# Two FFN down products: two column blocks at once, their first k tiles through seven products

## The chip, the cores and the metric

The kernel runs on one core of a Trainium2 chip. The metric is the device time of one execution in microseconds (us), lower is better. A core has TensorE (PE, matmuls, with its weight loads shown as PEld), VectorE (DVE), ScalarE (ACT), GpSimd (POOL) and SyncE (SP, which issues most transfers). Each engine works through its own instructions in the order that the program gives it, and waits on semaphores for the others.

## The reference

One layer of a streaming encoder, 256 tokens, width 2048, f32. What this case touches are its two half-step FFNs (hidden width 5632):

```python
def swiglu(h, w_gate, w_up, w_down):
    return (jax.nn.silu(h @ w_gate) * (h @ w_up)) @ w_down

x = x + 0.5 * swiglu(rms_norm(x, ffn1_norm[i]), ffn1_w_gate[i], ffn1_w_up[i], ffn1_w_down[i])
...   # input projection, S5 group, stick-breaking attention group, output projection
x = x + 0.5 * swiglu(rms_norm(x, ffn2_norm[i]), ffn2_w_gate[i], ffn2_w_up[i], ffn2_w_down[i])
...   # per-layer embedding, gated
```

## The kernel before

Every f32 matrix product is made of three fp32r products. An operand is split into a high part (a cast on ScalarE, L168) and a low part (source minus high part, on VectorE, L171), by `split`; then high x high, low x high and high x low are summed in PSUM. Tokens are two tiles of 128 (`TT = 2`), weights come in "quarters" of four k tiles by one column block of 512 (`raw`, 1 MB, three buffers), split in two halves of two k tiles each (`whi`, `wlo`, four buffers each). One half against both token tiles is 12 matmuls with 512 columns, one quarter 24. `gemm_block` does this for one column block: for each quarter it asks `act` for the split activations, loads and splits the quarter's weights, and calls `gemm_half` for each half. `step()` after each half lets work that was put off go ahead (`put_off(n, f)` calls f after n steps).

`ffn` has two parts. Gate and up: for each of 11 blocks f of 512 hidden columns, both products over 16 k tiles, then silu(gate) * up goes to `hh` and is turned into `hT` by transposes on VectorE and transfers (`turned`). Down: four column blocks n, each over 44 k tiles (11 quarters) with `gemm_block`; its activations are split anew from `hT` for every quarter of every column block (`act`, two buffers `hhi`, `hlo`); the result is added to the residual `xt` (L594) and `nxt.block(n)`, which turns and splits x for the next norm, is put off.

FFN 2 has a second way for gate and up (`sevens`), from block f = 1 on: `gemm_seven` takes the first quarter of gate and of up together as a 2 x 2 block product (two token tiles, two pairs of k tiles, two column blocks) and makes it with seven block products in place of eight, in the form of Winograd. For that it needs weight sums t1 to t4 (L459, VectorE), four sums of activation blocks (`sum_forms`, L409 to L426, made once for all f), and combinations of the seven results, which are left to `opened` and `gated`. Each product p is 6 matmuls: 4 with the high part of the weights, 2 with the low part. The remaining quarters accumulate into the same PSUM banks. FFN 1 runs the preparation of the S5 group beside gate and up (`bg`), and has no `sevens`.

The kernel's instructions are put in order, engine by engine, when it is built (`pin` keeps some in the order written). The PSUM has four banks for `acc` and two double banks for `aux`. The buffer tag "h" (`com`) has two buffers and serves `hh`, `sum_forms` and the norm's turned blocks; tags "nhi"/"nlo" have four, "hhi"/"hlo" two.

Of the kernel before, what the change touches and what calls it, by code (L numbers as in the profile page):

```python
# [33 lines left out]
def layer_kernel(ctx: ExitStack, tc: tile.TileContext, a: dict, shapes: dict, out: bass.AP):  # L34
# [29 lines left out]
    def uid(s):  # L64
        count[0] += 1
        return f"{s}_{count[0]}"
# [13 lines left out]
    def acc(s="acc"):  # L80
        return accp.tile([P, NB], F32, tag="acc", name=uid(s))
# [83 lines left out]
    def split(hi, lo, src, scale=None, pinned=False):  # L165

        if scale is None:
            copy = nc.scalar.copy(hi, src)  # L168
            if pinned:
                pin(copy)  # L170
            nc.vector.tensor_tensor(out=lo, in0=src, in1=hi.bitcast(F32), op=ALU.subtract)  # L171
        else:
            split_each(hi.unsqueeze(1), lo.unsqueeze(1), src.unsqueeze(1), [scale])
# [251 lines left out]
        split(*both, sums.rearrange("p (z t) -> p z t", z=4))  # L425
        return both  # L426

    def gemm_seven(act, sums, ws, n0, nkt, pool, first, second):

        raws = []  # L430
        for w in ws:
            raw = wp.tile([P, 4, NB], F32, tag="raw", name=uid("raw"), bufs=3)
            nc.sync.dma_start(raw, w[: 4 * P, n0 : n0 + NB].rearrange("(j p) n -> p j n", p=P))
            raws.append(raw)
        b11, b21, b12, b22 = (raw[:, 2 * h : 2 * h + 2, :] for raw in raws for h in range(2))
        parts = act(0)

        def whole(k, t):
            return [[u[:, 2 * k + j, t * P : (t + 1) * P] for j in range(2)] for u in parts]

        def summed(z):
            return [[u[:, z, j * P : (j + 1) * P] for j in range(2)] for u in sums]

        def product(ps, left, src, own, stop):
            hi, lo = (
                (pool if own else wp).tile([P, 2, NB], F32R, tag=s, name=uid(s), bufs=3 if own else None)
                for s in (("shi", "slo") if own else ("whi", "wlo"))
            )
            split(hi, lo, src)
            lh, ll = left  # L450
            for j in range(2):
                nc.tensor.matmul(ps, lhsT=lh[j], rhs=hi[:, j], start=j == 0, stop=False)  # L452
                nc.tensor.matmul(ps, lhsT=ll[j], rhs=hi[:, j], start=False, stop=False)  # L453
            for j in range(2):
                nc.tensor.matmul(ps, lhsT=lh[j], rhs=lo[:, j], start=False, stop=stop and j == 1)  # L455

        def add(x, y):
            t = pool.tile([P, 2, NB], F32, tag="sum", name=uid("sum"), bufs=2)
            nc.vector.tensor_tensor(out=t, in0=x, in1=y, op=ALU.add)  # L459
            return t  # L460

        p1, p2 = acc(), acc()
        product(p1, whole(0, 0), b11, False, True)
        product(p2, whole(1, 0), b21, False, False)
        step()
        t1 = add(b11, b12)
        p5 = acc()
        product(p5, summed(0), t1, True, True)
        t2 = add(t1, b22)
        p67 = aux()  # L470
        product(p67[:, :NB], summed(1), t2, True, True)
        step()
        t4 = add(t2, b21)
        p4 = acc()
        product(p4, whole(1, 1), t4, True, False)
        t3 = add(b12, b22)
        product(p67[:, NB:], summed(2), t3, True, True)
        step()
        p38 = aux()
        product(p38[:, :NB], summed(3), b22, False, False)  # L480
        step()
        put_off(0, first, p1, p67)
        for w, banks, fresh in ((ws[0], [p2, p4], False), (ws[1], [p38[:, :NB], p38[:, NB:]], True)):
            for k0 in range(4, nkt, 4):
                part = act(k0 // 4)
                for half in list(weight_halves(w, k0, 4, n0)):
                    begin = k0 == 4 and half[0] == 0
                    end = k0 + 4 >= nkt and half[0] == 1
                    for t in range(TT):
                        gemm_half({t: banks[t]}, (part, half), (t,), fresh and t == 1 and begin, end)  # L490
                    step()
            if not fresh:
                put_off(0, second, p2, p4, p5)
        return p38

    def ffn(i, xn, nxt, bg=None):
        wg, wu, wd = (a[f"ffn{i}_w_{s}"][0] for s in ("gate", "up", "down"))
# [22 lines left out]
        for f in range(NF):  # L520
# [5 lines left out]
            if sevens and f:  # L526
                sg, hh = com("sg"), com("h")
                gate_cols, up_cols = ([u[:, t * NB : (t + 1) * NB] for t in range(TT)] for u in (sg, hh))

                def opened(p1, p67, g=gate_cols, u=up_cols):  # L530
                    nc.scalar.copy(g[0], p1)
                    nc.vector.tensor_tensor(out=u[0], in0=p67[:, :NB], in1=g[0], op=ALU.add)
                    nc.vector.tensor_tensor(out=u[1], in0=p67[:, NB:], in1=u[0], op=ALU.add)

                def gated(p2, p4, p5, g=gate_cols, u=up_cols, hh=hh):
                    for z, (ps, other) in enumerate(((p2, g[0]), (p4, u[1]))):
# [3 lines left out]
                    nc.vector.tensor_tensor(  # L540
                        out=v, in0=p5.unsqueeze(1).to_broadcast([P, TT, NB]), in1=v, op=ALU.subtract
                    )

                p38 = gemm_seven(xn, sums, (wg, wu), f * NB, KD, sevens, opened, gated)
                nc.vector.tensor_tensor(out=hh, in0=p38, in1=hh, op=ALU.add)
                for t in range(TT):
                    nc.vector.scalar_tensor_tensor(
                        out=up_cols[t], in0=up_cols[t], scalar=xn.rs(t), in1=gate_cols[t], op0=ALU.mult, op1=ALU.mult
                    )
                put_off(2, turned, hp, f, hh)  # L550
                continue
# [36 lines left out]
            split(in_32(hi), in_32(lo), hT[k // 2][:, k % 2 * 4 : k % 2 * 4 + 4])  # L588
            return hi, lo

        for n in range(ND):
            ps = gemm_block(act, wd, n * NB, F // P)
            for t in range(TT):
                nc.vector.scalar_tensor_tensor(  # L594
                    out=xt[t][n], in0=ps[t], scalar=0.5, in1=xt[t][n], op0=ALU.mult, op1=ALU.add
                )
            put_off(0 if n == ND - 1 and n < nxt.early else 2, nxt.block, n)
        pools.close()


# [950 lines left out]
```

## Time and profile before

| | |
|---|---|
| median of 3 runs | 1870.7 us (1870.19 to 1871.19) |
| the profiled execution | 1872.24 us, its span 1870.4 us |
| mean granted clock | 1.0 |
| HBM read / written | 369.26 MB / 9.83 MB |
| instructions in the span | 23938 |

Stages, from the trace: gate and up of FFN 1 until 490 us, down of FFN 1 until 730, the mixing groups until 1054, gate and up of FFN 2 until 1523, its down product until 1763, then the per-layer embedding.

How to read it: a row of the page gives line, engine, operation, out<-in by the program's names, shapes, a count, then busy time, mean ns of one, and the idle time of the engine just before them with what ended it. A row of the timeline gives start and length in us, and in brackets the idle time before it with its releaser. A window gives each engine's busy time, and near its end the granted TensorE clock (1.00 is full), the share of the DMA engines and GB/s.

### The profile page before, as it was taken

Reading aid. Unit: us, or ns where it says so; the run is one execution under the profiler, and the core shown is the slowest. Engines: PE = TensorE matmul, PEld = TensorE weight load, DVE = VectorE, ACT = ScalarE, POOL = GpSimd, SP = SyncE. Lnnn points to the kernel's source line nnn. Section 1 sums busy time; section 2 is a strip of 40 time slices with the busy share of each in tenths; the row PEclk is TensorE's granted clock in tenths of the full one; section 3 lists DMA queues with packets and bytes.
Section 4 is the critical chain, followed back from the end, with each engine's and each line's share of the span. In section 5 each row is a group of like instructions: output and inputs, shape, how many; then the busy total and the mean of one; then the engine's idle time right before and its main releaser. Section 6 shows DMA issues by size and latency. Waiting matters only on the chain.

```text
span 1870.4 us, 23938 instructions
## 1 busy us (share of the span) xinstructions
PE 1859.4 (99%) x9134; PEld 1536.3 (82%) x9134; DVE 1310.4 (70%) x1527; ACT 996.5 (53%) x1151; POOL 50.4 (3%) x84
## 2 busy tenths in 40 slices
PE   9999999999999999999999999999999999999998
PEld 7888888888888888878888888888888888888887
DVE  8867665455576776687567678778787866777655
ACT  7444444444456665456695555445454555666554
POOL 0011000000000000010020000000000000000000
PEclk9999999999999999999999999999999999999999
DMA  8788867766655666675645666575666675656563
GB/s 323 242 278 268 267 208 222 231 217 200 217 196 199 212 199 244 185 248 163 222 147 189 218 205 221 203 220 186 203 205 208 225 228 203 204 202 212 189 224 124
DMA packets 230387, 400.06 MB, mean 214 GB/s; under 512 B 26401, under 2 KB 50337, under 8 KB 229985
## 3 DMA queue, kind: packets, MB, share of 16 engines
q1 hardware_dynamic: 227824, 392.81, 63.7%
q0 software_dynamic: 1728, 4.33, 0.7%
q8 instruction: 71, 1.16, 0.3%
q10 hardware_dynamic: 720, 1.41, 0.2%
q14 instruction: 44, 0.35, 0.1%
HBM read 369.26 MB, written 9.83 MB: 203 GB/s over the span
## 4 chain that ended last, share of the span: by engine, by line
PE 92%; ACT 3%; DVE 2%; DMA 1%; SPq 1%; issue 1%; POOL 0%; DVEq 0%; ACTq 0%; POOLq 0%
PE acc L292 26%; PE acc L297 26%; PE acc L293 26%; PE aux L293 3%; PE aux L292 3%; PE aux L297 3%; ACT whi L168 1%; SPq L1061 1%; PE acc L455 1%; DMA raw<-in_w_in 1%; PE aux L452 1%; PE acc L452 1%; PE acc L453 1%; PE aux L455 1%; PE aux L453 1%
## 5 line engine op out<-in xcount | busy, mean ns | idle before, releaser
L171 DVE TENSOR_TENSOR wlo<-raw,whi 128x1024 fp32r<-128x1024 f32 x656 | 798.2, 1224 | 458.9 <-ACT whi L168 455.3
L168 ACT CAST whi<-raw 128x1024 fp32r<-128x1024 f32 x656 | 686.2, 1053 | 758.7 <-PE acc L293 607.9
L292 PE MATMUL acc<-whi,nhi 128*128 128x512 f32 x1408 | 551.0, 391 | 1.2 <-ACT whi L260 0.5
L293 PE MATMUL acc<-whi,nlo 128*128 128x512 f32 x1408 | 548.2, 389 | 0.0
L297 PE MATMUL acc<-wlo,nhi 128*128 128x512 f32 x1408 | 384.4, 389 | 0.0
L292 PE MATMUL acc<-whi,hhi 128*128 128x512 f32 x816 | 317.6, 389 | 0.0
L293 PE MATMUL acc<-whi,hlo 128*128 128x512 f32 x816 | 317.5, 389 | 0.0
L292 PEld LDWEIGHTS acc<-whi,nhi 128*128 128x128 f32 x1408 | 264.3, 188 | 58.3 <-ACT whi L168 1.7
L297 PEld LDWEIGHTS acc<-wlo,nhi 128*128 128x128 f32 x1408 | 264.2, 188 | 55.6 <-DVE wlo L171 0.4
L293 PEld LDWEIGHTS acc<-whi,nlo 128*128 128x128 f32 x1408 | 264.4, 188 | 54.0
L297 PE MATMUL acc<-wlo,hhi 128*128 128x512 f32 x816 | 221.0, 389 | 0.0
L297 PEld LDWEIGHTS acc<-wlo,hhi 128*128 128x128 f32 x816 | 152.8, 188 | 32.5 <-DVE wlo L171 0.9
L293 PEld LDWEIGHTS acc<-whi,hlo 128*128 128x128 f32 x816 | 153.2, 188 | 32.0
L292 PEld LDWEIGHTS acc<-whi,hhi 128*128 128x128 f32 x816 | 153.1, 188 | 31.8
L171 DVE TENSOR_TENSOR hlo<-hT,hhi 128x1024 fp32r<-128x1024 f32 x88 | 107.1, 1218 | 0.0
L168 ACT CAST hhi<-hT 128x1024 fp32r<-128x1024 f32 x88 | 91.8, 1044 | 0.5 <-PE acc L455 0.4
L292 PE MATMUL aux<-whi,nhi 128*128 128x512 f32 x160 | 62.2, 389 | 0.0
L293 PE MATMUL aux<-whi,nlo 128*128 128x512 f32 x160 | 62.2, 389 | 0.0
L297 PE MATMUL aux<-wlo,nhi 128*128 128x512 f32 x160 | 49.3, 389 | 0.0
L171 DVE TENSOR_TENSOR slo<-sum,shi 128x1024 fp32r<-128x1024 f32 x40 | 48.6, 1214 | 0.4 <-ACT shi L168 0.2
L168 ACT CAST shi<-sum 128x1024 fp32r<-128x1024 f32 x40 | 42.1, 1052 | 11.5 <-DVE sum L459 11.4
L297 PEld LDWEIGHTS aux<-wlo,nhi 128*128 128x128 f32 x160 | 30.0, 188 | 6.2
(312 smaller groups left out, 1314.5 us busy)
## 6 DMA issues: line engine op xcount, KB each, us to landing
raw<-in_ffn_w_up SPq DMA_DIRECT2D x88, 1024.0 KB, 5.9
raw<-in_ffn_w_down SPq DMA_DIRECT2D x88, 1024.0 KB, 5.0
raw<-in_ffn_w_gate SPq DMA_DIRECT2D x86, 1024.0 KB, 5.4
raw<-in_w_in SPq DMA_DIRECT2D x32, 1024.0 KB, 5.5
raw<-in_w_out SPq DMA_DIRECT2D x16, 1024.0 KB, 5.1
raw<-in_w_ple_gate SPq DMA_DIRECT2D x16, 1024.0 KB, 5.1
hT<-mid SPq DMA_DIRECT2D x160, 64.0 KB, 5.0
h<-mid SPq DMA_DIRECT2D x176, 32.0 KB, 3.4
```

Of the source, the lines that this page charges most:

```text
L168: copy = nc.scalar.copy(hi, src)
L171: nc.vector.tensor_tensor(out=lo, in0=src, in1=hi.bitcast(F32), op=ALU.subtract)
L292: nc.tensor.matmul(ps[t], lhsT=lh, rhs=hi[:, j, cols], start=start and j == 0, stop=False)
L293: nc.tensor.matmul(ps[t], lhsT=ll, rhs=hi[:, j, cols], start=False, stop=False)
L297: nc.tensor.matmul(ps[t], lhsT=lh, rhs=lo[:, j, cols], start=False, stop=stop and j == 1)
L452: nc.tensor.matmul(ps, lhsT=lh[j], rhs=hi[:, j], start=j == 0, stop=False)
L453: nc.tensor.matmul(ps, lhsT=ll[j], rhs=hi[:, j], start=False, stop=False)
L455: nc.tensor.matmul(ps, lhsT=lh[j], rhs=lo[:, j], start=False, stop=stop and j == 1)
L1061: nc.sync.dma_start(zt[0][p1 : p1 + HC, z], sv[p0 : p0 + HC, r % 2 * 2 + r // 2])
```

## The change

`gemm_seven` becomes a class `Seven`, which can take several quarters ("chunks") of two column blocks through the seven products and accumulates them in the same banks; `column` does the rest of the quarters, of one column block at a time. The order of the products in a chunk was 1, 2, 5, 6, 4, 7, 3 and is 1, 5, 6, 4, 7, 2, 3. Gate and up of FFN 2 use it with one chunk, as before, but make the activation sums of two quarters. Down of both FFNs is done in two pairs of column blocks: the first pair with two chunks, the second with one; the split activations of a quarter serve both column blocks, except in the last six quarters of the second pair, where one column block is finished before the other and the activations are split for each. The sums of activations for a chunk of down are made when the chunk is reached. What was one addition to the residual for each column block and token tile is now four, spread over `opened` and the end of the pair.

```diff
-    def gemm_seven(act, sums, ws, n0, nkt, pool, first, second):
+    class Seven:
...
+        def bank(self, z):
+            if z not in self.banks:
+                if z in (1, 2, 4, 5):
+                    self.banks[z] = acc()
+                else:
+                    double = aux()
+                    for i, zz in enumerate((6, 7) if z in (6, 7) else (3, 8)):
+                        self.banks[zz] = double[:, i * NB : (i + 1) * NB]
...
+        def chunk(self, kb):
...
+            b11, b21, b12, b22 = (raw[:, 2 * h : 2 * h + 2, :] for raw in raws for h in range(2))
+            parts, sums = self.act(kb), self.sums(kb)
...
+            self.product(1, whole(0, 0), b11, False)
+            t1 = self.add(b11, b12)
+            self.product(5, summed(0), t1, True)
+            step()
+            t2 = self.add(t1, b22)
+            self.product(6, summed(1), t2, True)
+            t4 = self.add(t2, b21)
+            self.product(4, whole(1, 1), t4, True)
+            step()
+            t3 = self.add(b12, b22)
+            self.product(7, summed(2), t3, True)
+            self.product(2, whole(1, 0), b21, False)
+            step()
+            self.product(3, summed(3), b22, False)
+            step()
+            self.done += 1
+
+        def column(self, side, kbs):
+            banks = [self.bank(z) for z in ((2, 4), (3, 8))[side]]
+            w, n0 = self.ws[side]
+            for kb in kbs:
+                part = self.act(kb)
+                for half in list(weight_halves(w, 4 * kb, 4, n0)):
...
+                    for t in range(TT):
...
+                        gemm_half({t: banks[t]}, (part, half), (t,), begin, end)
                     step()
...
-                sums = sum_forms(xn(0))
+                sums = [sum_forms(xn(kb)) for kb in range(2)]
...
-        for n in range(ND):
-            ps = gemm_block(act, wd, n * NB, F // P)
+        def gather(x, ps, scale):
+            nc.vector.scalar_tensor_tensor(out=x, in0=ps, scalar=scale, in1=x, op0=ALU.mult, op1=ALU.add)
+
+        def opened(s, n):
+            sg = com("sg")
+            one, six = sg[:, :NB], sg[:, NB:]
+            nc.scalar.copy(one, s.bank(1))
+            nc.vector.tensor_tensor(out=six, in0=s.bank(6), in1=one, op=ALU.add)
+            gather(xt[0][n], one, 0.5)
             for t in range(TT):
-                nc.vector.scalar_tensor_tensor(
-                    out=xt[t][n], in0=ps[t], scalar=0.5, in1=xt[t][n], op0=ALU.mult, op1=ALU.add
-                )
-            put_off(0 if n == ND - 1 and n < nxt.early else 2, nxt.block, n)
+                gather(xt[t][n + 1], s.bank(5), 0.5)
+            gather(xt[0][n + 1], six, -0.5)
+            nc.vector.tensor_tensor(out=one, in0=s.bank(7), in1=six, op=ALU.add)
+            gather(xt[1][n], one, 0.5)
+            gather(xt[1][n + 1], one, -0.5)
+
+        last = F // P // 4
+        for n in range(0, ND, 2):
+            chunks, apart = ((2, 0), (1, 6))[n // 2]
+            parts = {}
+
+            def kept(kb):
+                if kb not in parts:
+                    parts.clear()
+                    parts[kb] = act(kb)
+                return parts[kb]
+
+            s = Seven(
+                kept, lambda kb: sum_forms(kept(kb)), ((wd, n * NB), (wd, (n + 1) * NB)), F // P, sevens, chunks
+            )
+            for kb in range(chunks):
+                s.chunk(kb)
+            put_off(0, opened, s, n)
+            for kb in range(chunks, last - apart):
+                for side in range(2):
+                    s.column(side, (kb,))
+            for side in range(2):
+                s.column(side, range(last - apart, last))
+                for t, z in enumerate(((2, 4), (3, 8))[side]):
+                    gather(xt[t][n + side], s.bank(z), 0.5)
+                m = n + side
+                put_off(0 if m == ND - 1 and m < nxt.early else 2, nxt.block, m)
```

In the text below, p1 to p7 are the seven products, t1 to t4 the weight sums, "forms" the four sums of activation blocks.

More of the change, by code (lines that the diff above doesn't have):

```diff
@@ L460, in add @@
             return t
[L462 to L488, printed above, removed]
+        def chunk(self, kb):
+            raws = []
+            for w, n0 in self.ws:
+                raw = wp.tile([P, 4, NB], F32, tag="raw", name=uid("raw"), bufs=3)
+                nc.sync.dma_start(
+                    raw, w[4 * kb * P : 4 * (kb + 1) * P, n0 : n0 + NB].rearrange("(j p) n -> p j n", p=P)
+                )
+                raws.append(raw)
+            b11, b21, b12, b22 = (raw[:, 2 * h : 2 * h + 2, :] for raw in raws for h in range(2))
+            parts, sums = self.act(kb), self.sums(kb)
+            def whole(k, t):
+                return [[u[:, 2 * k + j, t * P : (t + 1) * P] for j in range(2)] for u in parts]
+            def summed(z):
+                return [[u[:, z, j * P : (j + 1) * P] for j in range(2)] for u in sums]
+            self.product(1, whole(0, 0), b11, False)
[14 more added lines that the diff above has]
+            self.done += 1
```

72 lines of the change are left out of this document (42 added, 30 removed).

## The prediction

> **What bounds the kernel now.** I read the busy shares and the chain of waits first, then the stages of the two FFNs, then single instructions where a stage begins.
>
> ```profile
> PE 1859.4 (99%) x9134; PEld 1536.3 (82%) x9134; DVE 1310.4 (70%) x1527; ACT 996.5 (53%) x1151; POOL 50.4 (3%) x84
> PE 92%; ACT 3%; DVE 2%; DMA 1%; SPq 1%; issue 1%; POOL 0%; DVEq 0%; ACTq 0%; POOLq 0%
> ```
> ```profile
> 490.40:730.00 239.60, 239.60 (x1058) 198.39 (x1058) 169.67 (x159) 140.96 (x155) 2.33 (x4) 1.00 0.61 206
> 1080.00:1520.00 440.00, 439.43 (x1924) 359.49 (x1924) 350.93 (x338) 223.12 (x230) 0.00 (x0) 1.00 0.65 210
> 1523.30:1762.60 239.30, 239.30 (x1057) 198.18 (x1056) 170.26 (x159) 142.12 (x155) 0.00 (x0) 1.00 0.61 208
> ```
> The first fence is the page (busy time, chain), the second the windows of the down product of FFN 1, most of gate and up of FFN 2, and the down product of FFN 2 (columns: window, length, then busy time of PE, PEld, DVE, ACT, POOL, clock, DMA share, GB/s). TensorE is never out of work there; VectorE is busy for 71%, 80% and 71%. A busy TensorE says nothing of its pace, so here are two starts:
>
> ```profile
> 490.44 0.39 PE L292 MATMUL acc<-whi,hhi 128*128 128x512 f32 x1
> 729.80 0.39 PE L292 MATMUL acc<-whi,nhi 128*128 128x512 f32 x1
> ```
> The first is where down begins, the second where it has ended. The program puts 4 x 11 x 24 = 1056 matmuls between them: 239.36 / 1056 = **0.2267 us** each. So any matmul taken out of this stage is worth 0.2267 us, if what feeds the rest keeps up. What feeds it is a cast on ScalarE (the high part, L168) and a subtraction on VectorE (the low part, L171):
>
> ```profile
> 478.85 1.06 ACT L168 CAST whi<-raw 128x1024 fp32r<-128x1024 f32 x1 [1.67 <-PE acc L293]
> 479.94 1.22 DVE L171 TENSOR_TENSOR wlo<-raw,whi 128x1024 fp32r<-128x1024 f32 x1 [1.50 <-ACT whi L168]
> 482.66 1.23 DVE L171 TENSOR_TENSOR wlo<-raw,whi 128x1024 fp32r<-128x1024 f32 x1 [1.50 <-ACT whi L168]
> 485.38 1.23 DVE L171 TENSOR_TENSOR wlo<-raw,whi 128x1024 fp32r<-128x1024 f32 x1 [1.49 <-ACT whi L168]
> 488.10 1.23 DVE L171 TENSOR_TENSOR wlo<-raw,whi 128x1024 fp32r<-128x1024 f32 x1 [1.50 <-ACT whi L168]
> 490.41 1.41 DVE L580 SCALAR_TENSOR_TENSOR h<-acc,sm,sg 128x512 f32<-128x512 f32 x2 [1.09 <-PE acc L297]
> ```
> This is the timeline at the seam of up and down (T0 = 490.44). The four wts buffers hold the feeders back: the cast at 478.85 waits for matmuls of the half four before, and the low part of the last half of up is ready at 481.2, about 9 us ahead of T0. That lead of **8 to 9 us is all that VectorE can have**. The row at 490.41 is hh (L580): it waits for the last matmul of up, and all behind it on VectorE waits with it.
>
> **What is removed.** A chunk (four k tiles, two column blocks) takes 7 x 6 = 42 matmuls in place of 48. Down does two chunks in its first pair of column blocks and one in its second, so 3 x 6 x 2 FFNs = 36 matmuls go: 36 x 0.2267 = **-8.2 us**. Gate and up keep one chunk (`chunks = 1`), so there only the order moves. The act splits of down fall from 44 to 28 per FFN; that work is hidden now and is worth nothing by itself.
>
> **What is added** lands on VectorE, in the 19 us in which TensorE has the two chunks:
>
> ```profile
> L171 DVE TENSOR_TENSOR wlo<-raw,whi 128x1024 fp32r<-128x1024 f32 x656 | 798.2, 1224 | 458.9 <-ACT whi L168 455.3
> L168 ACT CAST whi<-raw 128x1024 fp32r<-128x1024 f32 x656 | 686.2, 1053 | 758.7 <-PE acc L293 607.9
> L171 DVE TENSOR_TENSOR slo<-sum,shi 128x1024 fp32r<-128x1024 f32 x40 | 48.6, 1214 | 0.4 <-ACT shi L168 0.2
> ```
> ```profile
> L414 DVE TENSOR_TENSOR h<-hhi,hlo x1: 1225/1225/1225, 1062.0 to 1062.0; 128x1024 f32<-128x1024 f32 x1
> L423 DVE TENSOR_TENSOR h<-h x2: 419/422/424, 1075.4 to 1075.7; 128x256 f32<-128x256 f32 x2
> L594 DVE SCALAR_TENSOR_TENSOR x<-acc,x x16: 680/686/693, 550.3 to 1763.2; 128x512 f32<-128x512 f32 x16
> ```
> ```profile
> 1182.47 1.22 DVE L171 TENSOR_TENSOR wlo<-raw,whi 128x1024 fp32r<-128x1024 f32 x1
> 1183.61 1.22 DVE L545 TENSOR_TENSOR h<-aux,h 128x1024 f32<-128x1024 f32 x1
> 1185.87 1.41 DVE L547 SCALAR_TENSOR_TENSOR h<-h,sm,sg 128x512 f32<-128x512 f32 x2
> 1187.20 1.22 DVE L459 TENSOR_TENSOR sum<-sum,raw 128x1024 f32<-128x1024 f32 x1
> 1188.33 0.71 DVE L203 STREAM_TRANSPOSE mid<-h 128x512 f32<-128x512 f32 x1
> 1188.96 1.18 DVE L459 TENSOR_TENSOR sum<-raw 128x1024 f32<-128x1024 f32 x1
> 1191.83 1.19 DVE L171 TENSOR_TENSOR slo<-sum,shi 128x1024 fp32r<-128x1024 f32 x1
> 1195.19 0.69 DVE L532 TENSOR_TENSOR h<-aux,sg 128x512 f32<-128x512 f32 x1
> 1195.80 1.22 DVE L171 TENSOR_TENSOR wlo<-raw,whi 128x1024 fp32r<-128x1024 f32 x1
> ```
> Back to back the starts are closer than the durations: 1.14 us for 128x1024 (1182.47 to 1183.61), 1.33 for the two halves of hh, 0.63 for a turn (1188.33 to 1188.96), 0.61 for a 128x512 sum, 0.34 for a 128x256 one (1075.4 to 1075.7). A chunk needs 7 low parts, 4 weight sums, the act split, hi+lo of the act, the split of its four sums (14 x 1.14) and four 128x256 sums (1.4): **17.3 us of VectorE against 42 x 0.2267 = 9.5 of TensorE**. Two quarters before cost it 6 x 1.14 = 6.8 against 10.9. Two chunks ask 34.7 against 19.0; hh, its turns and the eight gathers of `opened` add 7, and the column quarter behind them gives back 5: some 18 us short, less the 8 to 9 of lead. So about 9 us of stall per first pair is to be expected. The built program's order settles it place by place.
>
> **FFN 1, first pair.** VectorE's order in the changed program, with the time after T0 at which each is done (1.14, 0.66, 0.61, 0.34 us each; every high part on ScalarE is ready in time):
>
> ```
> before T0: low p1, t1, t2, low p2, low p5, low p6, t4   0.4
> hh x2 1.7 | hi+lo 2.8 | low p4 3.9 | t3 5.1 | turns x2 6.3
> low p3 7.4 | forms x3 8.4 | low p1' 9.6 | 4th form 9.9
> t1', hi+lo' 12.2 | low of the forms 13.4 | low p2' 14.5
> forms' x3, low p7, form' 17.0 | low p5', t2', low forms' 20.5
> ... low p4' 25.0 ... low p7' 29.6 | first column low 30.7
> 6 gathers 34.3 | low 35.5 | 2 gathers | low 37.8
> ```
> (A prime marks the second chunk.) TensorE's order is p1, p1', p5 and so on. It has p1 and the high half of p1' done at 2.3 and waits for the low part of p1' until 9.6: 7.3 us. p5 and p6 need the split of the sums, whose low part is done at 13.4, with 29 matmuls (6.6 us) issued: 6.9 us behind. Small waits follow to 21.4; from there TensorE is bound by itself. The 134 matmuls (30.4 us) up to the next column quarter end at 40.0: **+9.6 us**.
>
> **FFN 2, first pair.** Here p3's low part, t2 and hh with its scaling stand ahead, so low p1' is done at 10.9, the low of the forms at 16.8, low p7' at 33.0, and the 134 matmuls at 42.1: **+11.7**. The weights' loads stay as many, on the same queue:
>
> ```profile
> raw<-in_ffn_w_down SPq DMA_DIRECT2D x88, 1024.0 KB, 5.0
> ```
> Three raw buffers hold one and a half chunks, so the last load of the second chunk goes out when t4 is done (6.2) and lands at 11.2, just ahead of t1' (from 11.9). If it were late, all behind it would be.
>
> **Second pairs**, the same order in both FFNs. The forms can start before T0 (p1 and 4 sums are done at about -1.5), but behind T0 stand the gathers of the column block before, the splits, four turns of x for the next norm and the gathers of `opened`. TensorE waits for the high part of p4 (0.8), low p3 at 13.5 (2.0), the act split at 14.7 (0.5), low parts at 21.7 (0.9) and some tenths more: 92 matmuls (20.9) end at 26.2: **+5.3 each, 10.6**.
>
> **Gate and up of FFN 2.** A second set of sums is made, though one chunk uses one: on VectorE 1.14 for hi+lo, 1.14 for the low part and four of 0.34, together 3.7 us, and a cast on ScalarE. Round f = 0 hides them:
>
> ```profile
> 1060.00:1080.00 20.00, 20.00 (x90) 16.57 (x89) 14.23 (x24) 9.72 (x12) 0.00 (x0) 1.00 0.70 230
> ```
> VectorE is free for 5.8 of 20 us there; without that cover they would cost 3.7. The order matters at every second seam of f (four within gate and up), where p1's and p2's low parts precede t1:
>
> ```profile
> 1182.26 0.39 PE L452 MATMUL acc<-whi,hhi 128*128 128x512 f32 x1
> 1189.60 0.46 PE L452 MATMUL acc<-shi,hhi 128*128 128x512 f32 x1
> 1191.36 0.50 PE L452 MATMUL aux<-shi,nhi 128*128 128x512 f32 x1
> 1194.24 1.15 PE L297 MATMUL acc<-wlo,hhi 128*128 128x512 f32 x4
> ```
> Before, 50 matmuls (11.34 us) took 1182.26 to 1194.24, 11.98: 0.64 lost, since p1, p2, p5, p6, p3 and column matmuls filled the time until the last low part (1191.83). In the new order p4's high part is due after 25 matmuls (5.7) and ready at 7.3, and p7's low part (10.95) comes before any column: 42 matmuls (9.5) end at 11.4, 1.9 lost. 4 x (1.9 - 0.64) = **+5.0**; the bounds are 0 and 4 x 1.9 = 7.6. The other seams stay.
>
> **The clock.** The two waits of 7.3 and 8.6 us are longer than any in the body now:
>
> ```profile
> 974.10 0.71 PE L1190 MATMUL aux<-ones,sqg 128*128 128x128 f32 x4 [1.75 <-POOL sqg L1206]
> 1864.32 1.12 PE L1456 MATMUL aux<-e,diag 128*128 128x512 f32 x2
> 1868.00:1868.50 0.50, 0.00 (x0) 0.00 (x0) 0.00 (x0) 0.00 (x0) 0.00 (x0) 1.00 0.60 221
> 1868.50:1869.00 0.50, 0.00 (x0) 0.00 (x0) 0.00 (x0) 0.00 (x0) 0.00 (x0) 0.59 0.00 0
> 1869.00:1869.50 0.50, 0.00 (x0) 0.00 (x0) 0.00 (x0) 0.00 (x0) 0.00 (x0) 0.50 0.00 0
> ```
> The longest wait for another engine is 1.75 us, and the granted clock (third number from the end) stays at 1.00. At the end, where the last matmul ends at 1865.4, it falls to 0.50 near 1868.6, 3.1 us later. So both waits will lose it. How long it stays low no row shows. Below: it is back at once, 0. Above: the 74 matmuls left of the two chunks at half pace, 16.8 us per place. I take 3.1 us at half pace, as long as the fall took: 1.55 us lost per place, **+3.1**, with nothing absorbed, for TensorE has no slack after 21.4.
>
> [...]
>
> **The sum.** -8.2 + 9.6 + 11.7 + 10.6 + 5.0 + 3.1 = +31.8. The profiled execution took 1872.2 (span 1870.4), which gives 1904.0; the median of the three runs is 1.5 below it, so the forecast is **1902.5 us**. If each of the four stalls were a quarter smaller (8.0), seams and clock free (8.1), it would be 1886; a quarter larger, with seams at 7.6 and the clock at twice my value, 1916.
>
> **The rivals.**
>
> *The chunks stay hidden* (faster). Over a whole first pair VectorE fits: 9 quarters x 5.7 + 34.7 + 11 of gathers and turns is 97 us against 516 x 0.2267 = 117. If its work were spread over the pair, only the removal would count: 1870.7 - 8.2 = 1862.5. The shares of 71% speak for it. Against it stands the lead: it decides from about 18 us of work done ahead of T0, and the timeline shows 9, with hh in the middle of the queue. Chance 0.06.
>
> *Only the long wait counts.* VectorE catches up behind hh, as it does at the seams of gate and up, and TensorE loses the 7.3 and 8.6 us but no more: 1870.7 - 8.2 + 15.9 = 1878.4. For it: the second pairs have no single wait over 2 us. Against: after the long wait stands one for the split of the sums in the same queue, and the second pairs' four waits come out of the same prices. Chance 0.10.
>
> *The clock stays low through the chunks*: 2 x 16.8 in place of 3.1, 1933. For: the fall is certain after 7 us. Against: from 13.5 on TensorE is all but continuously busy. Chance 0.05.
>
> **How the numbers follow.** The forecast has 0.79, with 1884 to 1918 as its own range (nearly all of it); the two slower rivals have 0.15, the faster one 0.06. Reaching down to the second rival, 1877 to 1918 holds some 0.87; what is left out is the faster rival, the low clock and misses. This kernel's measurement tells about 0.2% (3.7 us) from no change. Faster 0.07 (the first rival and a little for what I overlooked), within 0.2% 0.03 (stalls that happen to equal the gain), slower 0.90.
>
> **What would show it.** In the profile after: TensorE idle for 7 to 9 us in one piece, released by the low part of the second chunk's first product, 2 us after down begins in each FFN, and the granted clock at 0.50 there and nowhere else; VectorE without a gap for some 30 us from T0; the two first pairs 7 and 9 us longer than 528 x 0.2267 = 119.7 (plus what the clock takes), the second pairs 4 longer; 36 matmuls fewer; at the seams of f, TensorE waiting 1.6 us for the high part of p4. The prediction is wrong if these waits are under 3 us, if VectorE begins the forms before hh, or if the long waits lie elsewhere, say on the weights' transfers or in round f = 0.

## The result and the profile after

The changed kernel takes **1911.7 us** (median of 4 runs, 1909.7 to 1912.7) against 1870.5 for the kernel before beside it: ratio 1.0219, 95% interval 1.0201 to 1.0236. The forecast was 1902.5 with a range of 1877 to 1918, so direction and range held, and the loss was 41 us where 31.8 were worked out. The profiled execution took 1911.8 us, its span 1910.0, which is 39.6 more than the span of before.

The page, its busy line and the chain that ended last by engine:

```profile
PE 1867.2 (98%) x9098; PEld 1534.0 (80%) x9098; DVE 1361.6 (71%) x1611; ACT 992.5 (52%) x1148; POOL 49.6 (3%) x84
PE 84%; DVE 9%; ACT 3%; DMA 2%; issue 1%; SPq 0%; POOL 0%; DVEq 0%; ACTq 0%; POOLq 0%
```

The 36 matmuls are gone (9134 to 9098). In the chain TensorE fell from 92% to 84% and VectorE rose from 2% to 9%: in some stretches VectorE now sets the end. The windows of the changed kernel say which. They are the down product of FFN 1, rounds f = 1 to 10 of FFN 2, and the down product of FFN 2 (columns as in the prediction):

```profile
490.54:744.78 254.24, 242.47 (x1039) 196.37 (x1038) 189.71 (x194) 135.25 (x151) 1.65 (x4) 0.97 0.58 197
1110.41:1546.10 435.69, 429.05 (x1861) 350.74 (x1861) 342.87 (x332) 217.41 (x224) 0.00 (x0) 0.99 0.63 205
1546.10:1801.94 255.84, 241.00 (x1039) 195.22 (x1038) 191.54 (x196) 137.90 (x152) 0.00 (x0) 0.98 0.58 196
```

The lengths were 239.36, 425.8 (1097.51 to 1523.30) and 239.36 before. VectorE is busy for only 75% in down, and TensorE is idle for 12 and 15 us of it all the same. TensorE's waits in the changed kernel, by what released them (total us, times, the longest):

```profile
PE acc L463 <- DVE wlo L171: 15.7, 2, 8.6
PE acc L460 <- ACT shi L168: 6.4, 6, 1.5
PE aux L463 <- DVE wlo L171: 3.9, 2, 2.0
PE acc L460 <- ACT nhi L168: 3.3, 2, 2.3
```

The first and fourth belong to the first pairs, the second is the high part of t4 (four seams of f and two small ones), the third the low part of p3 in the second pairs. TensorE's timeline at the two first pairs:

```profile
490.54 0.39 PE L460 MATMUL acc<-whi,hhi 128*128 128x512 f32 x1
...
492.58 0.39 PE L461 MATMUL acc<-whi,hlo 128*128 128x512 f32 x1
500.16 1.22 PE L463 MATMUL acc<-wlo,hhi 128*128 128x512 f32 x2 [7.19 <-DVE wlo L171]
502.32 0.79 PE L460 MATMUL acc<-shi,nhi 128*128 128x512 f32 x1 [0.94 <-ACT nhi L168]
502.91 0.63 PE L460 MATMUL aux<-shi,nhi 128*128 128x512 f32 x1
```
```profile
1557.08 1.22 PE L463 MATMUL acc<-wlo,hhi 128*128 128x512 f32 x2 [8.55 <-DVE wlo L171]
1560.63 0.80 PE L460 MATMUL acc<-shi,nhi 128*128 128x512 f32 x1 [2.33 <-ACT nhi L168]
```

TensorE does p1 and the high half of p1', then stands; the matmuls that follow take 0.63 (the row at 502.91) in place of 0.39 us, and the granted clock is 0.50 in the window from 502 to 503 (last section). What VectorE does in that time, from its own timeline:

```profile
490.84 1.40 DVE L613 SCALAR_TENSOR_TENSOR h<-acc,sm,sg 128x512 f32<-128x512 f32 x2
492.15 1.22 DVE L414 TENSOR_TENSOR h<-hhi,hlo 128x1024 f32<-128x1024 f32 x1
...
495.56 1.30 DVE L203 STREAM_TRANSPOSE mid<-h 128x512 f32<-128x512 f32 x2
496.78 1.19 DVE L171 TENSOR_TENSOR wlo<-raw,whi 128x1024 fp32r<-128x1024 f32 x1
497.88 0.75 DVE L423 TENSOR_TENSOR h<-h 128x256 f32<-128x256 f32 x2
498.55 0.42 DVE L423 TENSOR_TENSOR h<-h,h 128x256 f32<-128x256 f32 x1
498.88 1.22 DVE L171 TENSOR_TENSOR wlo<-raw,whi 128x1024 fp32r<-128x1024 f32 x1
500.02 0.42 DVE L423 TENSOR_TENSOR h<-h,h 128x256 f32<-128x256 f32 x1
```

It is the queue of the prediction, row by row: hh (L613) at T0, the join of the activations (L414), the turns (L203), the forms (L423), and the low part of p1' at 498.88, ended at 500.1, T0 + 9.6. So far the forecast holds. Whether these rows also are the *reason* in the way it was put is another question, and the experiments answer it in part against it.

By stages, the 39.6 us are:

| stage | forecast | measured |
|---|---|---|
| FFN 1, first pair (490.54 to 618.72) | -2.7 + 9.6 + 1.55 = +8.5 | +8.5 |
| FFN 1, second pair (to 744.78) | -1.4 + 5.3 = +3.9 | +6.4 |
| mixing stage | 0 | -2.2 |
| FFN 2, rounds f = 1 to 10 | +5.0 | +9.9 |
| FFN 2, first pair (1546.10 to 1677.31) | -2.7 + 11.7 + 1.55 = +10.6 | +11.5 |
| FFN 2, second pair (to 1801.94) | +3.9 | +5.0 |
| the rest | 0 | +0.5 |

### The profile page after: what moved, and what is told of

Its sections match the earlier page's. It is cut to its first block, busy times and chain, and to the rows that moved or that the text cites. A ratio compares the mean times of both kernels' runs of the same rounds, so it can differ in the third digit from the quotient of the medians.

```text
span 1910.0 us, 23845 instructions
## 1 busy us (share of the span) xinstructions
PE 1867.2 (98%) x9098; PEld 1534.0 (80%) x9098; DVE 1361.6 (71%) x1611; ACT 992.5 (52%) x1148; POOL 49.6 (3%) x84
## 4 chain that ended last, share of the span: by engine, by line
PE 84%; DVE 9%; ACT 3%; DMA 2%; issue 1%; SPq 0%; POOL 0%; DVEq 0%; ACTq 0%; POOLq 0%
PE acc L292 20%; PE acc L293 20%; PE acc L297 20%; PE aux L293 6%; PE aux L292 6%; PE aux L297 6%; DVE wlo L171 2%; DVE slo L171 2%; DVE sum L467 1%; PE acc L460 1%; PE acc L461 1%; ACT whi L168 1%; PE acc L463 1%; PE aux L463 1%; PE aux L460 1%
## 5 line engine op out<-in xcount | busy, mean ns | idle before, releaser
L292 PE MATMUL acc<-whi,hhi 128*128 128x512 f32 x416 | 162.3, 392 | 1.0 <-ACT whi L168 1.0
L293 PE MATMUL acc<-whi,hlo 128*128 128x512 f32 x416 | 162.8, 392 | 0.2 <-DVE hlo L171 0.2
L292 PE MATMUL aux<-whi,hhi 128*128 128x512 f32 x384 | 150.0, 391 | 0.0
L293 PE MATMUL aux<-whi,hlo 128*128 128x512 f32 x384 | 149.6, 390 | 0.0
L297 PE MATMUL acc<-wlo,hhi 128*128 128x512 f32 x416 | 126.8, 390 | 0.0
L297 PE MATMUL aux<-wlo,hhi 128*128 128x512 f32 x384 | 118.5, 390 | 1.2 <-DVE wlo L171 1.2
L292 PEld LDWEIGHTS acc<-whi,hhi 128*128 128x128 f32 x416 | 78.3, 188 | 18.6 <-ACT whi L168 1.9
L293 PEld LDWEIGHTS acc<-whi,hlo 128*128 128x128 f32 x416 | 78.6, 189 | 17.4 <-DVE hlo L171 1.0
L297 PEld LDWEIGHTS acc<-wlo,hhi 128*128 128x128 f32 x416 | 78.1, 188 | 16.8 <-DVE wlo L171 0.5
L292 PEld LDWEIGHTS aux<-whi,hhi 128*128 128x128 f32 x384 | 72.2, 188 | 15.7 <-ACT whi L168 0.7
```

What stands on the lines that cost most here:

```text
L292: nc.tensor.matmul(ps[t], lhsT=lh, rhs=hi[:, j, cols], start=start and j == 0, stop=False)
L293: nc.tensor.matmul(ps[t], lhsT=ll, rhs=hi[:, j, cols], start=False, stop=False)
L297: nc.tensor.matmul(ps[t], lhsT=lh, rhs=lo[:, j, cols], start=False, stop=stop and j == 1)
```

## The experiments

Each ratio is against the kernel before, run beside it (its medians there were 1871.2 to 1872.7). "Loss" of a pair below is its length less 0.2267 us for each of its matmuls.

**1. Sharing without the seven products.**

```diff
-            chunks, apart = ((2, 0), (1, 6))[n // 2]
+            chunks, apart = ((0, 0), (0, 6))[n // 2]
...
-            put_off(0, opened, s, n)
```

> The down products take two column blocks at once with their activations split once, but no k tile goes through seven products there (44 x 48 / 2 = 1056 matmuls per FFN again); gate and up of FFN 2 stay as in the changed kernel. Theory A (the loss in down comes from the chunks alone, the sharing is free): down takes 239.4 us in both FFNs as in the kernel before, no wait of over 1 us within it; what is left of the loss is the seams of gate and up, 9.9 us by the windows: 1870.5 + 9.9 = 1880, less up to 2 if the mixing stage is again shorter; range 1876 to 1883. Theory B (holding four banks and going to and fro between two column blocks itself costs TensorE or the weight queue time): down stays several us above 239.4 and the kernel is above 1886.

Measured: 1877.6 us, 1.0031 (1.0019 to 1.0044). Windows of down, of the ten rounds, and of down:

```profile
490.91:730.27 239.36, 239.36 (x1057) 198.20 (x1056) 151.88 (x142) 125.45 (x139) 1.65 (x4) 1.00 0.63 206
1095.78:1527.08 431.30, 425.22 (x1862) 348.36 (x1860) 338.54 (x327) 215.05 (x221) 0.00 (x0) 1.00 0.65 209
1527.08:1766.44 239.36, 239.36 (x1058) 198.20 (x1056) 152.46 (x143) 125.92 (x139) 0.00 (x0) 1.00 0.62 207
```

Down takes 239.36 us, to the hundredth what it took before. Two column blocks at once cost TensorE nothing, and the act splits that are saved (VectorE's 169.7 to 151.9) bring nothing: theory A. All of the loss in down is the chunks'.

**2. The old order of the seven products, in gate and up only.**

```diff
+            if self.last == KD // 4 - 1:
+                self.product(1, whole(0, 0), b11, False)
+                self.product(2, whole(1, 0), b21, False)
+                step()
+                t1 = self.add(b11, b12)
+                self.product(5, summed(0), t1, True)
...
+            else:
                 self.product(1, whole(0, 0), b11, False)
                 t1 = self.add(b11, b12)
                 self.product(5, summed(0), t1, True)
...
```

> The changed kernel with the seven products of gate and up of FFN 2 in the order of the kernel before (1, 2, 5, 6, 4, 7, 3); down is left as changed. Theory A (the new order puts t4's high part before TensorE's third product too late, 2.28 us at each odd seam): rounds f = 1 to 10 fall from 435.7 to 425.8 us, the waits for the high part of t4 go, 1911.7 - 9.9 = 1902, range 1900 to 1904. Theory B (the seams lose because VectorE also makes the sums of a second k tile and because down's pools hold buffers, whatever the order): the rounds stay above 432 and the time above 1908.

Measured: 1905.4 us, 1.0177 (1.0163 to 1.0191), 1.4 above A's range; the rounds took 428.8, where A said 425.8 and B over 432. The odd seams are cured: no wait for t4's high part is left there, and rounds f = 3, 5, 7, 9 take 42.9 as before. Of the 6.9 us by which the rounds fell, 3.1 are stretches of half clock behind two of those waits, 3.42 us at 0.50 each (last section); the windows of the rounds show a clock of 0.99 in the changed kernel and 1.00 here. But round f = 1 now takes 44.8, with a new wait of 1.52 us. Run 8, with the same order and one set of sums, has no such wait and takes 42.8 there; the next run tells what the second set does.

**3. One set of activation sums in gate and up.**

```diff
-                sums = [sum_forms(xn(kb)) for kb in range(2)]
+                sums = [sum_forms(xn(0))]
```

> The changed kernel without the sums of the second k tile that the first round of gate and up of FFN 2 makes and nobody reads (eight 128x256 sums and differences and two 128x1024 splits and their joins fewer, some 7 us of VectorE once). Theory A (round f = 1 lost 1.25 us because VectorE was late by these): f = 1 falls from 43.66 to about 42.4 and the time by about 1.2 to 1910.5. Theory B (nothing waits for them): 1911.7, within 0.5.

Measured: 1908.4 us, 1.0195 (1.018 to 1.0211). Round f = 1 falls from 43.53 to 42.28 us, the 1.25 us of theory A (the 43.66 in the expectation is round f = 0; f = 1 had 43.53). The unread sums are not hidden by round f = 0, they push VectorE back into the next. But the span fell by 3.8, more than A allows: the ten rounds took 431.3 in place of 435.7. The other 3.1 of these are the clock of the two profiled executions (0.99 and 1.00 in the windows of the rounds), see the last section.

**4. The chunks of down away from the seams.**

```diff
-            for kb in range(chunks):
-                s.chunk(kb)
-            put_off(0, opened, s, n)
-            for kb in range(chunks, last - apart):
-                for side in range(2):
-                    s.column(side, (kb,))
+            for kb in range(last - apart):
+                if kb in ((2, 6), (4,))[n // 2]:
+                    s.chunk(kb)
...
+                else:
+                    for side in range(2):
+                        s.column(side, (kb,))
```

> The changed kernel with its chunks moved away from the seams: quarters 2 and 6 of the first pair of column blocks and quarter 4 of the second; the same 36 matmuls fewer, the gate and up of FFN 2 as changed. Theory A (a chunk asks 17.3 us of VectorE against 9.5 of TensorE, and VectorE's lead of 8 to 9 us covers one such deficit when it has built up again, so only two chunks in a row at a seam stall): each pair of down loses its stall, 128.2 + 126.1 + 131.2 + 124.6 falls to 4 x 119.7 less 8.2 = 470.6, that is 39.5 us less: 1872, range 1868 to 1880, and no step of lower clock in down. Theory B (the lead can't be used, because the buffers of the sums (two) and of the high and low parts (three) hold the splits of a chunk back until TensorE reaches it): each of the six chunks keeps about the stall of a second pair, 1.36 + 3.9 = 5.3 us, 1872 + 6 x 5.3 = 1904, range 1895 to 1910.

Measured: 1878.2 us, 1.0033 (1.0021 to 1.0044). The same 36 matmuls fewer, the same work on every engine, and the windows of down are

```profile
490.60:729.08 238.48, 237.12 (x1039) 194.25 (x1038) 193.05 (x197) 137.49 (x153) 1.65 (x4) 1.00 0.62 207
1527.46:1765.93 238.47, 237.04 (x1040) 194.24 (x1038) 193.56 (x198) 138.83 (x153) 0.00 (x0) 1.00 0.62 207
```

254.2 and 255.8 have become 238.5 twice, and the clock stays at 1.00. A chunk in the middle meets a VectorE that is ahead, and the lead is used: theory A. Not all is won, 238.5 against 1038 x 0.2267 = 235.3; TensorE still waits four times for 0.7 us behind the chunk of the second pairs.

**5. One chunk in place of two at the seam.**

```diff
-            chunks, apart = ((2, 0), (1, 6))[n // 2]
+            chunks, apart = ((1, 0), (1, 6))[n // 2]
```

> The changed kernel with one chunk in place of two at the start of the first pair of each FFN, order and seams otherwise as changed; 12 matmuls more, +2.7 us. Theory A (the long wait is the deficit of two chunks one behind the other, 2 x 7.8 us against one lead of 8 to 9): with one chunk the deficit is 7.8 plus some 4 for hh and its turns, the lead covers most; the waits of 7.2 and 8.6 us fall to 1 to 4, each first pair takes 120 to 125 us in place of 128.2 and 131.2, the kernel 1893 to 1902. Theory B (the wait belongs to the seam: hh, its turns and the sums of the activations are late for whichever chunk comes first): waits of 6 us or more stay, 1908 to 1914.

Measured: 1915.0 us, 1.0226 (1.0211 to 1.0242), 1 above B's range. Theory A, the forecast's own account, fails. TensorE at the first pair of FFN 1 and of FFN 2, then two rows of VectorE in FFN 1:

```profile
491.85 0.61 PE L463 MATMUL acc<-wlo,hhi 128*128 128x512 f32 x2
501.97 0.79 PE L460 MATMUL acc<-shi,nhi 128*128 128x512 f32 x1 [9.51 <-ACT nhi L168]
...
1561.78 0.79 PE L460 MATMUL acc<-shi,nhi 128*128 128x512 f32 x1 [13.01 <-ACT nhi L168]
```
```profile
491.24 1.40 DVE L613 SCALAR_TENSOR_TENSOR h<-acc,sm,sg 128x512 f32<-128x512 f32 x2
...
500.42 0.42 DVE L423 TENSOR_TENSOR h<-h,h 128x256 f32<-128x256 f32 x1
```

The waits grew to 9.5 and 13.0 us. They end with the split of the *first* chunk's own activation sums (`nhi`). VectorE's queue from hh to those sums is as long as with two chunks (hh starts at 491.24, the last form of the first chunk at 500.42; with two, 490.84 and 500.02); all that the second chunk did was to give TensorE the high half of p1' to do meanwhile. The loss of FFN 1's first pair is 11.2 with two chunks (128.2 - 516 x 0.2267) and 11.2 with one (129.6 - 522 x 0.2267): the second chunk costs nothing there. In FFN 2 it is 14.2 with two and 15.7 with one.

**6 and 7. The sums made before the seam.** In FFN 2 only, with two chunks and with one; join and sums work in a weight buffer in place of the two of the tag "h". Both also leave out the second set of sums, as in 3.

```diff
...
+        def prepare():
+            ready["parts"] = act(0)
+            ready["sums"] = sum_forms(ready["parts"], True)
...
+            if f == NF - 1 and not bg:
+                put_off(10, prepare)
```

> The changed kernel with one set of sums in gate and up, and with the activations' split and sums for the first chunk of down in FFN 2 alone made during the last round of gate and up, in a buffer that the dropped second set leaves free. FFN 1 is left as it was, for comparison. It tells what the long wait of FFN 2 (8.55 us, first pair 131.3 us against 117.0 for its matmuls) is made of. Theory A (as predicted: the total of VectorE's work for two chunks, hh and the gathers): 3.7 us of that total are moved away, the wait only moves to the second chunk's sums (4 to 6 us for their high part), first pair 127 to 128. Theory B (only the way from T0 to the first split of the sums counts, what comes later is done in time): the first pair falls to 119 to 122, no wait over 2 us.

> The same with one chunk in place of two at the start of the first pairs (12 matmuls more in all). With one chunk FFN 2's first pair took 134.1 us with a wait of 13.0 us for the split of the sums, 118.3 for its matmuls. Both theories have that wait gone now. Theory A has one chunk fit within the lead once its sums are made ahead: 119 to 121, a wait of at most 2 us. If instead hh and its turns are what holds the queue, whatever the sums do, low parts of p4 or p7 are late by 3 us or more and the pair stays at 123 or above. FFN 1's first pair stays at 129.6.

Measured: 1905.1 us, 1.0174 (1.016 to 1.0188), with two chunks, and 1900.4 us, 1.0152 (1.0138 to 1.0166), with one. The first pair of FFN 2 in windows, for 6 (its first 31 us, then the whole) and then for 7:

```profile
1543.76:1575.00 31.24, 26.28 (x105) 18.64 (x104) 31.24 (x35) 17.25 (x19) 0.00 (x0) 1.00 0.49 161
1543.76:1669.17 125.41, 120.14 (x518) 96.03 (x516) 93.10 (x93) 63.77 (x64) 0.00 (x0) 1.00 0.56 189
```
```profile
1545.85:1667.97 122.12, 120.60 (x523) 98.95 (x522) 83.14 (x81) 60.12 (x60) 0.00 (x0) 0.99 0.58 194
```

With the runs before, FFN 2's first pair loses

| | sums behind hh | sums made ahead |
|---|---|---|
| two chunks | 131.2 - 117.0 = 14.2 | 125.4 - 117.0 = 8.4 |
| one chunk | 134.1 - 118.3 = 15.7 | 122.1 - 118.3 = 3.8 |

Neither theory of run 6 holds alone: 125.4 lies between 119 to 122 and 127 to 128. The table reads as two limits side by side. Behind hh, the queue to the first sums decides, and a second chunk adds nothing. With that taken away, the total of VectorE's work shows: with two chunks it is busy for all of the first 31.24 us, while TensorE has 26.28, and the second chunk costs 4.6, or some 6 without the stretch of half clock that run 7 met (0.99 in its window) and run 6 did not (1.00). Of the 3.8 that are left with one chunk, 1.5 are the wait for t4's high part, the one of the odd seams, and some 1.6 the stretch of half clock behind it (from 1553.8 to 1556.8 its matmuls take 0.63 in place of 0.39 us, 0.43 from start to start in place of 0.23); so the expected 119 to 121 was missed by what the order and the clock cost.

**8 to 12. Towards a better kernel.** All have the old order in gate and up, one set of sums, and spaced chunks.

8, that and nothing else:

> Chunks of down at quarters 2 and 6 of the first pair and 4 of the second, gate and up of FFN 2 in the old order of products, and the sums of the unread second k tile left out: all three findings of the runs so far together. Theory A (the three losses are independent): against the spaced kernel 5 odd seams give back 44.40 - 42.90 = 1.5 each and round f = 1 1.2: 1874.0 - 8.7 = 1865.3 for the profiled span (the kernel before 1870.4), so 0.2 to 0.4% under the kernel before measured beside it. Theory B (a chunk in down that no longer stalls and the old order at the seams fight for the same lead of VectorE): less than half of it, no faster than the kernel before.

1869.9 us, 0.9987 (0.9978 to 0.9996), span 1868.0: 6.0 us of the 8.7 came between the two profiled executions, 8.3 between the medians. Run 4 was profiled in the fastest of its six executions (1875.8 to 1879.5), which lost nothing to the clock (mean granted clock 1.0), and its rounds have four odd seams, not five. The rounds took 426.6.

9, three chunks in the first pairs, at quarters 2, 5 and 8:

> As the last, with three chunks in the first pair (quarters 2, 5 and 8), one in the second: two chunks more in all, 12 matmuls fewer, -2.7 us if VectorE carries them. A chunk asks 10.5 us more of VectorE than the column quarters it replaces, less 1.4 of time; an ordinary pair of quarters leaves it 10.9 - 6.8 = 4.1. Two ordinary ones between chunks give back 8.2 against 7.8 short. Theory A (supply and demand over the distance decide): just carried, 1862.6 for the span, waits under 0.7 us. Theory B (the lead must be built up in full before each chunk): waits of 1 to 3 us at quarters 5 and 8, and no gain over two chunks, 1865 to 1869.

1870.0 us, 0.9985 (0.9976 to 0.9993), no difference that these intervals tell from run 8; the wait for the activations' split in the second pairs grew from 0.75 to 1.13 us.

10, the chunk of gate and up moved from the first quarter of a round to the second:

```diff
-                s.chunk(0)
...
-                s.column(0, rest)
+                for side in range(2):
+                    s.column(side, (0,))
+                s.chunk(1)
+                put_off(0, opened, s)
+                s.column(0, range(2, KD // 4))
                 put_off(0, gated, s)
-                s.column(1, rest)
+                s.column(1, range(2, KD // 4))
...
-                sums = [sum_forms(xn(kb)) for kb in range(2)]
+                sums = {1: sum_forms(xn(1))}
```

> As the first of these four, with the chunk of gate and up of FFN 2 moved too, from the first to the second of the four quarters of a round, so that no round begins with seven products. Theory A (a chunk away from the seam meets VectorE with its lead): the odd seams lose nothing, ten rounds take 421.7 to 424 in place of 427, 1862 for the span. Theory B (in gate and up VectorE is busy for 80%, one quarter does not build up the lead, and hh and its turns now fall into the same stretch): the wait only moves into the round, at t4's or a low part, 1865 to 1872.

1866.5 us, 0.9967 (0.9954 to 0.9979). The ten rounds take 423.0 us with no wait in them: theory A, also at 81% of VectorE.

11, the gathers of `opened` in the second pairs put off:

```diff
-                        put_off(0, opened, s, n)
+                        put_off(6 if n else 0, opened, s, n)
```

> As the kernel with all chunks away from the seams, and with the eight gathers behind the chunk of the second pairs put off by six half quarters more. There TensorE waited 0.75 for the split of the activations and 0.69 for a low part, twice each within 5 us of those gathers. If the gathers in VectorE's queue are the cause, the four waits go and the time falls by 2.9 us (1864.4 to 1861.5 for the span); if the chunk alone is the cause, the waits stay where they are and the time too.

**1862.0 us, 0.9946 (0.9932 to 0.9959)**, better than both kernels. Its windows, and all that TensorE waits for by 0.8 us or more:

```profile
490.95:727.42 236.47, 236.47 (x1039) 194.41 (x1038) 192.93 (x197) 137.62 (x153) 1.65 (x4) 1.00 0.62 209
1093.00:1516.05 423.05, 423.05 (x1862) 348.65 (x1861) 342.37 (x331) 216.54 (x223) 0.00 (x0) 1.00 0.66 211
1516.05:1752.47 236.42, 236.42 (x1039) 194.38 (x1038) 193.48 (x198) 138.92 (x153) 0.00 (x0) 1.00 0.62 209
```
```profile
PE aux L1282 <- POOL sqg L1298: 1.8, 1, 1.8
PE aux L235 <- POOL ones L126: 1.1, 1, 1.1
PE acc L292 <- ACT whi L260: 0.8, 1, 0.8
```

The first lies in the mixing stage, the others at the kernel's start. VectorE's busy time is within 6 us of the changed kernel's (1355.8 to 1361.6); what has changed is its place and, in gate and up, its order.

12, run 11 with the three chunks of run 9:

> As the last kernel, with the chunks of the first pairs at quarters 2, 5 and 8 in place of 2 and 6: 12 matmuls fewer in all, 2.7 us. Without the deferred gathers this step moved the span by 0.8 us only (1868.0 to 1867.2). Theory A (what it lost there was lost to the gathers of the second pairs, which are put off here): 1860.6 - 2.7 = 1857.9 for the span, no wait over 0.5 us in down. Theory B (VectorE, which was busy for 195 of 240 us in down, has no lead left for a chunk every third quarter): waits of 0.5 to 2 us at or behind quarters 5 and 8, span 1859.5 to 1863.

1861.1 us, 0.9946 (0.9932 to 0.9959), span 1858.8 (between theory A's 1857.9 and theory B's 1859.5) and down 235.4 twice, with no wait of 0.2 us or more in it: 1.8 of the 2.7 in the span, and nothing that the intervals tell from run 11.

## Why the prediction was right, and where not

- **36 matmuls, -8.2.** Right in number; what 0.2267 us each is worth shows where nothing else waits, in run 11, where down is 2.9 us shorter in each FFN (4.1 for 18 matmuls, less 1.2 that went in tenths).
- **First pairs, +9.6 and +11.7.** Place, length of the waits (7.19 for 7.3, 8.55 for 8.6) and lengths of the pairs (+8.5 for 8.5, +11.5 for 10.6) came as worked out from the order of the program. That FFN 1 agrees to the tenth is luck: the clock took 0.5 more there than forecast, the stalls as much less. VectorE had one gap of 1.2 us (before 507.2) in the 30 us that were to have none. The reason given above it fails: "Two chunks ask 34.7 against 19.0 ... So about 9 us of stall per first pair is to be expected." By that sum one chunk should have waited 1 to 4 us (the expectation of run 5), and it lost as much as two. What sets the loss is the row in the middle of the same list: hh can't start before the last matmul of up, and the forms of the first chunk stand behind it and its turns. The total is a second limit, near in size, which shows only without the first (run 6). What holds the forms there was not separated: their result takes one of the two buffers of the tag "h", which hh uses too, and runs 6 and 7 changed place and buffer at once.
- **Second pairs, +3.9 each.** +6.4 and +5.0. The wait for p3's low part was 1.93 and 1.96 as forecast (2.0). In FFN 1 a stretch of half clock came on top (0.50 from 632.22 to 635.64).
- **Seams of f, +5.0.** The wait for t4's high part is there (1.48 us for the 1.6 named), runs 2 and 10 confirm that order and place cause it. Slightly mis-sized: without the clock the four odd rounds lost 6.0 (44.4 against 42.9 each) and the even ones gave back 0.5, so 5.5, not 5.0; the unread sums cost 1.25 more in f = 1, where the prediction had them hidden by round f = 0 (run 3).
- **The clock, +3.1.** This step failed in part. The two long waits cost some 4.1 (10 matmuls each at 0.43 in place of 0.23 us behind them), near enough; but "there and nowhere else" is wrong. It also fell behind waits of 1.93, 1.48 and 1.48 us in this execution, each time to 0.50 for 3.42 us (last section), 1.6 us lost each: 4.8.
- **Not foreseen**: the mixing stage became 2.2 us shorter. Most of it is one hole in the matmuls of the kernel before, where the profile shows no engine that it waited for:

```profile
822.90 0.45 PE L959 MATMUL aux<-ua,m 64*64 64x64 f32 x13 [1.45 <-issue]
```

The changed kernel has none in the mixing stage, run 5's has one of 1.38 there, before other matmuls (L1169). What makes it come and go stays open; no run was spent on it.

Together: 31.8 + 5.8 for the clock + 1.25 for the sums + 0.5 at the seams - 2.2 in mixing is 37.2. Of the 2.4 left to the span's 39.6, 0.9 and 1.1 lie in the second pairs, where no run took them apart, and the others are tenths.

The rivals: "the chunks stay hidden" was wrong for this program and right in its condition, for run 11 spreads the same work and takes the 1862 us that it gave, though a part of that is gate and up's (423.05 against 425.8 in the rounds). "Only the long wait counts" fell with the second pairs, "the clock stays low through the chunks" with 4.1 us.

## What to carry to other kernels

Work that trades matmuls for vector work should not begin at a seam, where the vector engine's queue holds something that must wait for the matrix engine's last result: put it a few tiles later, as here, where the same work then cost next to nothing (1.2 us per FFN in run 11). A busy share of 75% says nothing there; ask for each product what stands ahead of its inputs in the queue, and check a sum of work against a version with half of it. Leave out results that nobody reads even where an engine looks idle, and spread what comes due behind such a block.

## What the hardware showed that was not expected

In the profiled execution of the changed kernel the granted clock fell to half and came back five times in the two FFNs. One-microsecond windows (length, PE busy, clock, DMA share, GB/s):

```profile
495.00:496.00 1.00, 0.00 (x0) 0.85 0.19 72
505.00:506.00 1.00, 1.00 (x4) 0.53 0.07 14
632.00:633.00 1.00, 1.00 (x3) 0.61 0.27 62
635.00:636.00 1.00, 1.00 (x5) 0.68 0.93 352
1291.00:1292.00 1.00, 1.00 (x4) 0.50 0.93 344
1294.00:1295.00 1.00, 1.00 (x5) 0.79 0.87 276
1379.00:1380.00 1.00, 1.00 (x5) 0.87 0.90 250
1383.00:1384.00 1.00, 1.00 (x5) 0.92 0.99 358
1553.00:1554.00 1.00, 0.00 (x0) 0.91 0.24 86
1564.00:1565.00 1.00, 1.00 (x5) 0.97 0.14 33
```

If the clock is 0.50 until it is 1, the rises are at 505.94, 635.64, 1294.42, 1383.16 and 1564.06 (0.79 is 0.42 us at half and 0.58 at full), and by the same reckoning the falls are at 495.70, 632.22, 1291.00, 1379.74 and 1553.82. In the two long holes it fell while TensorE stood, and was low for 10.24 us each time; behind three short holes it was low for 3.42 us. The rises lie 129.70, 658.78, 88.74 and 180.90 us apart. The stretch of 3.42 goes 37.9 times into 129.70; taken as 38 times it is 3.413, which goes 193.0, 26.0 and 53.0 times into the other distances and 3.0 times into 10.24. That the changes of this execution lie whole multiples of 3.413 us apart is an estimate from these windows; what sets it was not shown.

Not every short hole was followed by a fall. The wait of 1.48 us for t4's high part comes four times in the changed kernel. The clock fell behind the two that end at 1290.42 and 1378.67, 0.6 and 1.1 us later, and was 1.00 behind the two that end at 1203.69 and 1466.89. In runs 6 and 7 it comes nine times, and behind five of them the matmuls take 0.63 us in place of 0.39. Run 3, in which the round that fell at 1291.00 comes 0.9 us earlier, has the same wait of the same length,

```profile
1289.55 0.50 PE L460 MATMUL acc<-shi,hhi 128*128 128x512 f32 x1 [1.48 <-ACT shi L168]
```
```profile
1290.00:1291.00 1.00, 1.00 (x6) 1.00 0.64 207
1291.00:1292.00 1.00, 1.00 (x6) 1.00 1.03 401
```

and the clock stays at 1.00. What makes the difference was not shown. The two stretches of half clock in rounds f = 5 and 7 are nearly all of the extra 3.1 us of the changed kernel's profiled execution: from one of these waits to the next it takes 86.73 us (1203.69 to 1290.42), and 88.25 and 88.22 where the clock fell in between.

Run 4's six executions took 1875.8 us at a mean granted clock of 1.0 up to 1879.5 at 0.997. Only one execution of each kernel was profiled, so where the others lost it is not shown. How long a hole must be was not settled either: 1.48 us was enough twice in the changed kernel, and 1.96 us (ended at 1690.54, the clock 1.00 from 1690 to 1700) was not.
